# Other places in SBUF for the operands of a hybrid encoder layer's matmuls

## The chip, the core and the metric

The kernel runs on one core of a Trainium2 chip. The metric is the device time of one execution in microseconds (us); lower is better. Engines are named as in the profile: PE is TensorE's matmul, PEld its weight load, DVE VectorE, ACT ScalarE, POOL GpSimd, SP SyncE.

## What is computed

One layer over a sequence of 512 tokens of width 1024, all in float32. Three parts follow each other, each added to the residual stream `x`; shift, scale and gate of each part come from a conditioning vector.

```python
def swiglu(h, w_in, w_out):
    gate, up = jnp.split(h @ w_in, 2, axis=-1)
    return (jax.nn.silu(gate) * up) @ w_out
...
h = modulate(rmsnorm(x, norm_ffn1[l]), sh1, sc1)
x = x + 0.5 * g1[:, None, :] * swiglu(h, w_ffn1_in[l], w_ffn1_out[l])
h = modulate(rmsnorm(x, norm_mix[l]), sh2, sc2)
qa, ka, va, qb, kb, vb, ga, gb = jnp.split(h @ w_in[l], SPLIT_POINTS, axis=-1)
...
ya = window_gqa_sink(qa, ka, va, sink_a[l]) @ w_branch_a[l]
...
yb = ob @ w_branch_b[l]
merged = jax.nn.sigmoid(ga) * ya + jax.nn.sigmoid(gb) * yb
x = x + g2[:, None, :] * (merged @ w_out[l])
h = modulate(rmsnorm(x, norm_ffn2[l]), sh3, sc3)
x = x + 0.5 * g3[:, None, :] * swiglu(h, w_ffn2_in[l], w_ffn2_out[l])
```

The hidden width of each SwiGLU is 2816. `window_gqa_sink` is attention within a window of 128 with 8 query heads and 2 key heads; `ob` comes from a differential attention of 4 heads over all 512 tokens.

## The kernel before

**Products.** Every large product is made of float32 values that are split into a high and a low part; a product is three matmuls (high by high, high by low, low by high), the lines 456 to 458 in `two` and 173 to 175 in `mm3`. In the first FFN from its fourth pair of column blocks on, and in nearly all of the second, the products of blocks follow Strassen's scheme in seven products of 2 x 2 blocks: a `Unit` has the quarters `a11`, `a12`, `a22` of its weights and the sums `s1` to `s4`, and the operand's quarters `b11` to `b22` with the sums `n1`, `n2`, `t3`, `t4` (`OPERAND` says which goes with which; `n1` goes with `s1`). Such matmuls move 256 columns; the plain ones move 512. A product takes 6 matmuls for each step of depth, so 24 at depth 4.

**Places of the weights.** The split weights lie in two tiles, `high` and `low`, of five slots each. `high_low` hands the slots out in turn; a set is one slot's pair. A set starts, in float32 values, at `i * 1024 + min(i, 2) * GAP + aside` for slot `i`, where `GAP` is 64 and the caller gives `aside`: 16 (`ASIDE`), 24 (`TURN`), 64 (`FAR`) or 0. So slots 2, 3 and 4 are 1024 apart, and a set with an `aside` ends in the next slot's first values.

**Places of the operands.** Operands lie in tiles called `b8` (`b` in the profile) and, some, in `u4` tiles (`u`) and in `ka`. The first FFN's `n1` is in two `u4` tiles (line 605); in the second FFN `n1` is in `u4` too, and of what the second output product reads, the last places are `ka` and `u4`. In bytes of a partition, modulo 256, `high`, `low`, `b8` and `ka` tiles start at 64 and `u4` tiles at 160 (from the order and the sizes in which the pool's tiles are laid out).

**The difference.** While TensorE streams one matmul's operand, the next matmul's weights are loaded. The text calls "difference" the start of those weights less the start of that operand, in bytes modulo 256. An `aside` of 16 under a `b8` operand gives 64; under `n1` in `u4` tiles it gives 224; `TURN` gives 96 under a `b8` operand, `aside` 0 or `FAR` gives 0. Where the operand moves out of `high` and `low` and the weights are in `b8` (the projections of lines 1192 to 1213), the sign turns: `aside` 16 gives 192.

**Order of work.** The first FFN's input products alternate with its output products, which move 512 columns (`Out1`, FAR): output chunks start near 110, 181, 252 and 324 us, and behind each of the first three the next unit's product `s2` is the first of 256 columns. The last four output columns (`LAST_1`) are done by halves of 256 columns, from 340 us, then the first three gates, whose weights are in `u4` tiles (to 377 us). Then come the projections of the mixers, gates and attention (to about 645 us; the window mixer's keys and queries by `project_pairs`, lines 1198 to 1215, from 454 to 499 us), among which small transposes (line 1270) are strewn; then the rest of the branch products, the mixer's output columns (`MIX_ASIDES`; the last two by halves, from 701 us), and the second FFN from 713 us. In that the first unit is `Plain` (two halves of a plain product, sets `a11` and `a21` at `TURN`), beside it `lead`, and from 743 us on units in Strassen's scheme, with two `out_unit`s from 812 us on, two from 927 us on and two at the end. TensorE's order is written out by hand in the FFNs and at the boundaries between the parts; elsewhere a scheduler orders each engine's instructions by priority and by what must wait for what.

Of the kernel before, what the change touches and what calls it, by code (L numbers as in the profile page):

```python
# [18 lines left out]
P = 128  # L19
# [77 lines left out]

RAW, HILO, F2 = 5, 5, 8

ASIDE, TURN, GAP = 16, 24, 64  # L100

FAR = 64


BRANCH_ASIDES = (ASIDE, TURN, ASIDE, ASIDE), (ASIDE,) * 4
MIX_ASIDES = 0, 0, 0, 0, 0, 0, ASIDE, ASIDE

CHUNKS = (range(0, 6), range(6, 12), range(12, 16), range(16, 22))
PLAIN, LAST_1 = 3, 4
# [24 lines left out]
def layer(ctx: ExitStack, tc: tile.TileContext, a: dict):  # L134
# [13 lines left out]
    def xt():  # L148
        return sbuf("x", [P, T], F32, 8)
# [16 lines left out]
    def keep(shape, nm, dt=F32):  # L166
        return sb.tile(shape, dt, name=nm, tag=nm, bufs=1)
# [28 lines left out]
    def high_low(n=1024, aside=0, holder=None):  # L196
        while turn[0] % HILO in holders:
            turn[0] += 1
        i = turn[0] % HILO
        turn[0] += 1  # L200
        if holder:
            holders[i] = holder
        i = i * 1024 + min(i, 2) * GAP + aside
        return tuple(t[:, i : i + n] for t in parts)

    def let_go(holder):
# [24 lines left out]
    sub8, lam_s, nlam = (keep([P, n], nm) for nm, n in (("sub8", 1), ("lam_s", 2), ("nlam", 1)))  # L231
    rqa, ccol = keep([P, NT, 8], "rqa"), small(NC)
    x = [xt() for _ in range(NC)]
    parts, modv = [], []
    for nm, n in (("high", 6), ("low", 0)):
        parts.append(keep([P, HILO * 1024 + 2 * GAP + ASIDE], nm, F32R))
        modv += [keep([P, NC], f"mod{v}") for v in range(n)]

    def load_by(t, src, n):
# [9 lines left out]
        return w  # L249


    begin, begins, norms = keep([P, 6 * NC], "begin"), {}, {SC1: NORM1, SC2: NORM2, SC3: NORM3}

    def mod_begin(v):
        if v in (SH1, SH2, SH3):
# [204 lines left out]
    class Unit:  # L460
# [12 lines left out]
        MAKE = {"s1": 5, "a11": 3, "a12": 2, "s2": 4, "s4": 2, "s3": 2, "a22": 3}  # L473
        asked, length = ("s1", "a11", "a12", "a22"), 1.0

        in_order = turned = by_columns = ()
        spare, roomy, apart, more = ("s1",), (), (), {"s1": ("s2", "a11"), "s2": ("s4", "a12"), "a11": ("s3", "a21")}

        def place(self, q):
# [14 lines left out]
        def prepare(self, q):  # L494

            if q in self.ready:
                return
            self.ask(q)
            n = self.depth * 2 * P
            if q in self.apart:  # L500
                both = b8().rearrange("p a b -> p (a b)")
                hi, lo = both[:, 0:n], both[:, 1024 : 1024 + n]
            else:
                hi, lo = high_low(n, TURN if q in self.turned else ASIDE, (self, q))
            t = self.at[q]
            with tc.issue_after(copied[0]) if q in self.in_order and copied else nullcontext():
                split_from(hi, lo, t)
            self.ready[q] = hi, lo
            if q in self.more:
                s, src = self.more[q]  # L510
                G.dma_start(t, self.srcs[src], accum_op=ALU.add)
                self.at[s] = t
# [103 lines left out]
    cact = [sbuf("ka", [P, D], F32, 1)]  # L616
    hh, hl = new_h()
    modv += [keep([P, NC], f"mod{v}") for v in range(len(modv), 9)]
    nc.scalar.dma_start(ccol, a["c"])
    tc.keep_in_program_order(nc.scalar.dma_start(par, a["par"]))  # L620
    for c in range(NC):
# [2 lines left out]
    with tc.manual_schedule(engines=BOUND | {mybir.EngineType.SP, mybir.EngineType.Pool}):  # L624
# [24 lines left out]
        def first_loads(k):  # L649
            n = 1 if k else 2  # L650
            scale = mod_load(SC1, k, n=n)
            if k == 0:
                kept.append(keep([P, NT], "pos", I32))
            shift = mod_load(SH1, k, n=n) if k == 0 else None
            raw = sbuf("raw", [P, 1024], F32, RAW)
            load_by(raw, a["w1s"][k], n)
            w1[k] = [scale, shift or mod_load(SH1, k), raw]
# [227 lines left out]
    def in_unit1(p):  # L885
        srcs = {q: a["w1u"][p - PLAIN, i] for i, q in enumerate(("a11", "a12", "a21", "a22"))}
        u = Unit(srcs, 4, h1_operand, in_post1, p % 2)
        u.p, u.in_order = p, ('s2', 's4')
        return u

    class Out1:
# [17 lines left out]
        def prepare(self, m):  # L909
            if m not in self.ready:  # L910
                self.ask(m)
                aside = FAR if not self.by_halves(m) else TURN if m < NC - LAST_1 + 2 else ASIDE
                if self.final and m == 0:
                    while turn[0] % HILO != 1:
                        turn[0] += 1
                t = self.ready[m] = high_low(self.depth * P, aside, (self, m))
                with tc.issue_after(copied[0]):
                    split_from(*t, self.at[m])
# [196 lines left out]
    def load_main(src, aside=0):  # L1115

        raw = sbuf("raw", [P, 1024], F32, RAW)
        nc.sync.dma_start(raw, src)
        hi, lo = high_low(aside=aside)
        halves = slice(0, 512), slice(512, 1024)  # L1120
        for j in halves:
            S.copy(hi[:, j], raw[:, j])
        for j in halves:
            S.activation(lo[:, j], raw[:, j], AF.Identity, scale=-1.0)
        G.dma_start(lo, src, accum_op=ALU.add)
        return hi, lo
# [68 lines left out]
                    yield MM3 * n / T  # L1195
        then(out)

    def project_pairs(srcs, then):

        n = 2 * P  # L1200
        out = [bank("acc") for _ in range(2)]
        for u, src in enumerate(srcs):
            wh, wl = load_main(src, ASIDE)
            for t in range(NT):
                ht = slice(t * P, (t + 1) * P)
                po = out[t // 2][:, t % 2 * n : (t % 2 + 1) * n]
                for i in range(4):
                    k = 4 * u + i
                    w = slice(i * n, (i + 1) * n)
                    first, last = k == 0 and t % 2 == 0, k == NC - 1 and t % 2 == 1  # L1210
                    PE.matmul(po, hh[k][:, ht], wh[:, w], start=first, stop=False, skip_group_check=True)
                    PE.matmul(po, hh[k][:, ht], wl[:, w], start=False, stop=False, skip_group_check=True)
                    PE.matmul(po, hl[k][:, ht], wh[:, w], start=False, stop=last, skip_group_check=True)
                    yield MM3 / 2
        then(out)
# [11 lines left out]
    def gates(more=lambda: True):  # L1227
        while gate_next[0] < 16 and more():
            j = gate_next[0]
            gate_next[0] += 1  # L1230

            wh, wl = load_main(a["w_gate"][j], ASIDE * (j == EARLY_A))
            out = bank("acc")
            for k in range(NC):
                o = k * P
                mm3(out, wh[:, o : o + P], wl[:, o : o + P], hh[k], hl[k], k == 0, k == NC - 1)
                yield MM3
            gate_end(j, out)
# [423 lines left out]
            turns["w"] = (b, g * nk + kc + 1)  # L1662


    def branch(w, j0, o_h, o_l, then, load, r=FULL[0], asides=(0, 0, 0, 0)):
        for u in range(4):
            with tc.issue_after(banded_last[0]):
                wh, wl = load(w[u], aside=asides[u])
            for i in range(2):
                j = 2 * u + i  # L1670
                g = f2()[:, r]
                nc.sync.dma_start(g, gate_scr[j0 + j][:, r])
                y = bank("acc")[:, r]
                for k in range(4):
                    o = k * 256 + i * P
                    mm3(y, wh[:, o : o + P], wl[:, o : o + P], o_h[:, k, r], o_l[:, k, r], k == 0, k == 3)
                    yield MM3 * (r.stop - r.start) / T
                then(j, g, y, r)

    def main():  # L1680
# [4 lines left out]
        while later or asked:  # L1685
            column(later)
        tables_a()
        yield from project_pairs([a["w_kva"][u] for u in range(2)], keys_a)
        for g in range(2):
            yield from project_pairs([a["w_qa"][2 * g + u] for u in range(2)], lambda ps, g=g: queries_a(ps, g))  # L1690
        yield from gates(lambda: done["b"] < NT)
# [19 lines left out]

        for i, r in enumerate(HALVES):
            line.drain(lambda: done["a"] >= 2 * i + 2)
            yield from branch(a["w_ya"], 0, *wa["o"], then_b, load_halves, r, BRANCH_ASIDES[i])

    mix = []
    line.run(main())
# [85 lines left out]
    def out_unit(part, g, final):  # L1803
        def post(c, v, u):
            n, t = int(c[1]) - 1, int(c[2]) - 1
            for j in range(2):
                m = 4 * g + 2 * n + j
                xr = x[m][:, HALVES[t]]
                V.scalar_tensor_tensor(xr, v[:, j * H : (j + 1) * H], modv[G3][:, m : m + 1], xr, ALU.mult, ALU.add)
                if final:  # L1810
                    nc.sync.dma_start(a["out"][m][:, HALVES[t]], xr)

        r = slice(part.start * 2 * P, part.stop * 2 * P)
        srcs = {q: a["w2o"][g, i][:, r] for i, q in enumerate(("a11", "a12", "a21", "a22"))}
        return Unit(srcs, len(part), act_operand, post, g)

    units = [in_unit(p) for p in range(NH)]

# [19 lines left out]
            V.scalar_tensor_tensor(g, g, -1.0, self.bank[1, t], ALU.mult, ALU.mult)  # L1838

    plain = units[0] = Plain(units[0].srcs, 4, h_operand, None, 0)  # L1840
    plain.turned = ("a11", "a21")
    lead = units[1]
    lead.spare, lead.roomy, lead.apart = ("s1", "a11", "a12"), ("a22",), ("s1", "a12")
    for u in units[1:]:
        u.in_order = ("s2", "s3", "s4", "a22") if u is lead else ("s1", "s2", "s3", "s4", "a22")
    units[2].MAKE = {**Unit.MAKE, "s2": 3}
    lead.tags = {"w": "acc", "v": "tp"}
    with tc.manual_schedule(engines={mybir.EngineType.Pool}):
        for u, q in ((plain, "a11"), (plain, "a21"), (lead, "a11")):
# [249 lines left out]
```

## Time and profile before

| | |
|---|---|
| runs | 1039.71 us median of 3 (1039.4 to 1041.84) |
| the profiled execution | 1039.97 us, of which the span 1038.2 |
| PE busy | 1030.8 us (99%), granted clock 1.00 |
| PEld busy | 951.1 us (92%) |
| DVE, ACT, POOL busy | 786.9, 583.9, 162.5 us |
| DMA | 220.92 MB, 213 GB/s over the span |

The span reaches from the first to the last instruction in the profile. Matmuls overlap, and their ends are modelled, so a matmul's duration in the profile is longer than the distance from its start to the next one's start. What a stretch costs is therefore read from starts: in the view of windows each row gives a stretch (from and to, in us from the span's start), its length, then PE's busy time with the count of matmuls that touch the stretch, the granted clock, the DMA engines' share and GB/s. In the timeline a row is start, length, engine, line and operation.

### The profile page before, as it was taken

The page shows a single profiled execution, that of the slowest core. Times are in us where ns is not written, and L with a number is a line of the kernel's source. Part 1 is how long each engine was busy: PE and PEld are TensorE (multiplying, and loading weights), DVE is VectorE, ACT ScalarE, POOL GpSimd, SP SyncE. Part 2 cuts the span into 40 slices and gives each one's busy share as a digit, 9 for nine tenths or more (in the row PEclk, how much of TensorE's full clock was granted, in tenths as well). Part 3 has the DMA queues.
Part 4 walks back from the last instruction along what each step waited for, and adds up shares of the span by engine and source line. Part 5 has one row for each costly group of instructions (what it writes and reads, how often), then busy time and mean ns, then how long its engine had stood idle before and what let it go on. Part 6 is the DMA issues. An engine that isn't in the chain of part 4 may idle for free.

```text
span 1038.2 us, 18851 instructions
## 1 busy us (share of the span) xinstructions
PE 1030.8 (99%) x7346; PEld 951.1 (92%) x7346; DVE 786.9 (76%) x1456; ACT 583.9 (56%) x1014; POOL 162.5 (16%) x190
## 2 busy tenths in 40 slices
PE   9999999999999999999999999999999999999998
PEld 7789899899999998899888888989999999999998
DVE  7786667567796679859782598976899777877877
ACT  6665335244364343667785856525867546654553
POOL 1101110110110100543333101001112112112210
PEclk9999999999999999999999999999999999999999
DMA  9977787966884459796737944974498998989974
GB/s 360 356 238 203 233 231 209 257 166 205 253 203 133 152 192 410 236 288 139 186 69 190 254 134 151 364 252 104 94 237 191 243 229 207 224 223 214 211 156 112
DMA packets 70377, 220.92 MB, mean 213 GB/s; under 512 B 8464, under 2 KB 13200, under 8 KB 70288
## 3 DMA queue, kind: packets, MB, share of 16 engines
q1 hardware_dynamic: 47808, 146.52, 39.0%
q0 software_dynamic: 19344, 68.70, 35.9%
q10 hardware_dynamic: 3136, 4.51, 1.2%
q8 instruction: 57, 0.93, 0.3%
q14 instruction: 32, 0.26, 0.1%
HBM read 209.46 MB, written 10.23 MB: 212 GB/s over the span
## 4 chain that ended last, share of the span: by engine, by line
PE 94%; DMA 2%; DVE 2%; ACT 2%; issue 0%; SPq 0%; DVEq 0%; ACTq 0%
PE acc L457 7%; PE acc L458 7%; PE acc L456 7%; PE sc L457 6%; PE sc L458 6%; PE sc L456 6%; PE sc L173 5%; PE sc L174 5%; PE sc L175 5%; PE acc L173 5%; PE acc L175 5%; PE acc L174 5%; PE tp L1270 2%; DMA raw<-w1s 2%; PE acc L1192 2%; PE acc L1194 2%
## 5 line engine op out<-in xcount | busy, mean ns | idle before, releaser
L189 ACT CAST high<-raw 128x1024 fp32r<-128x1024 f32 (+2 forms) x176 | 158.2, 913 | 152.9 <-PE sc L174 40.4
L189 DVE TENSOR_TENSOR low<-raw,high 128x1024 fp32r<-128x1024 f32 (+2 forms) x176 | 183.2, 1050 | 42.1 <-ACT high L189 40.8
L456 PE MATMUL acc<-b,high 128*128 128x256 f32 x508 | 140.9, 277 | 0.0
L457 PE MATMUL acc<-b,high 128*128 128x256 f32 x508 | 140.7, 277 | 0.1
L458 PE MATMUL acc<-b,low 128*128 128x256 f32 x508 | 140.6, 277 | 0.0
L457 PE MATMUL sc<-b,high 128*128 128x256 f32 x500 | 138.2, 276 | 0.0
L456 PE MATMUL sc<-b,high 128*128 128x256 f32 x500 | 138.1, 276 | 0.0
L458 PE MATMUL sc<-b,low 128*128 128x256 f32 x500 | 138.1, 276 | 0.0
L189 ACT CAST high<-u 128x1024 fp32r<-128x1024 f32 (+1 forms) x73 | 75.5, 1035 | 50.5 <-PE sc L174 20.2
L189 DVE TENSOR_TENSOR low<-u,high 128x1024 fp32r<-128x1024 f32 (+1 forms) x73 | 87.6, 1200 | 20.4 <-ACT high L189 18.8
L173 PE MATMUL sc<-b,high 128*128 128x512 f32 (+1 forms) x272 | 97.5, 358 | 0.0
L174 PE MATMUL sc<-b,high 128*128 128x512 f32 (+1 forms) x272 | 97.2, 357 | 0.0
L175 PE MATMUL sc<-b,low 128*128 128x512 f32 (+1 forms) x272 | 97.1, 357 | 0.0
L457 PEld LDWEIGHTS acc<-b,high 128*128 128x128 f32 x508 | 95.5, 188 | 0.4 <-DVE b L1883 0.3
L456 PEld LDWEIGHTS acc<-b,high 128*128 128x128 f32 x508 | 95.5, 188 | 0.3 <-ACT f L534 0.2
L458 PEld LDWEIGHTS acc<-b,low 128*128 128x128 f32 x508 | 95.4, 188 | 0.0
L458 PEld LDWEIGHTS sc<-b,low 128*128 128x128 f32 x500 | 93.9, 188 | 0.0
L456 PEld LDWEIGHTS sc<-b,high 128*128 128x128 f32 x500 | 93.9, 188 | 0.0
L457 PEld LDWEIGHTS sc<-b,high 128*128 128x128 f32 x500 | 93.9, 188 | 0.0
L173 PE MATMUL acc<-b,high 128*128 128x512 f32 (+1 forms) x240 | 89.0, 371 | 0.0
L175 PE MATMUL acc<-b,low 128*128 128x512 f32 (+1 forms) x240 | 86.7, 361 | 0.0
L174 PE MATMUL acc<-b,high 128*128 128x512 f32 (+1 forms) x240 | 86.5, 361 | 0.0
(397 smaller groups left out, 2715.9 us busy)
## 6 DMA issues: line engine op xcount, KB each, us to landing
u<-w_mod SPq DMA_DIRECT2D x38, 512.0 KB, 8.3
b<-w_mod SPq DMA_DIRECT2D x32, 512.0 KB, 5.5
raw<-w2i SPq DMA_DIRECT2D x31, 512.0 KB, 5.4
u<-w2i POOLq DMA_DIRECT2D x31, 512.0 KB, 6.7
raw<-w1u SPq DMA_DIRECT2D x24, 512.0 KB, 7.1
u<-w1u POOLq DMA_DIRECT2D x24, 512.0 KB, 7.1
raw<-w1o SPq DMA_DIRECT2D x24, 384.0 KB, 4.4
raw<-w_gate SPq DMA_DIRECT2D x16, 512.0 KB, 5.2
```

Source lines behind the costliest of these rows:

```text
L173: PE.matmul(out, wh, xh, start=first, stop=False)
L174: PE.matmul(out, wh, xl, start=False, stop=False)
L175: PE.matmul(out, wl, xh, start=False, stop=last)
L189: last = S.copy(hi, src), V.tensor_tensor(lo, src, f(hi), ALU.subtract)
L456: PE.matmul(out, wh[:, s], xh, start=first and j == 0, stop=False, skip_group_check=True)
L457: PE.matmul(out, wh[:, s], xl, start=False, stop=False, skip_group_check=True)
L458: PE.matmul(out, wl[:, s], xh, start=False, stop=last and j == 1, skip_group_check=True)
L1192: PE.matmul(out[t][:, 0:n], hh[k][:, ht], wh[:, o : o + n], start=k == 0, stop=False)
L1194: PE.matmul(out[t][:, 0:n], hl[k][:, ht], wh[:, o : o + n], start=False, stop=k == NC - 1)
L1270: PE.transpose(tp[:, j * P : (j + 1) * P], src, ident)
```

## The change

It moves operands and weights in SBUF; no instruction is added or taken away, and what is computed stays.

- Small tiles are added or widened ("pad1", "pad2", `begin`, "pos"), so that `u4` tiles start where `b8` tiles do, at 64 modulo 256, and `high` and `low` start at 0. The DMA scratch goes from 4096 to 2048 bytes.
- The slots of `high` and `low` are all 1088 values apart, and 16 is added to every `aside`. So an `aside` of 16 still gives 64 under `b8`, and now under `n1` too; 0 still gives 0.
- `FIRST`, -8, gives 224. It goes to: `s1` of the first Strassen unit (224 before as well, being `n1`'s), the sets behind the 512 columns of the first FFN's output (`s2`, 64 before), the first set of the window branch's first half (64 before), the second to last mixer output column (64 before), `a11` of the second FFN's third unit (64), and `s1` of the first output unit of each of the second FFN's first two parts (64).
- `ENTRY`, 32, gives 128: the first of the four last output columns of the first FFN (96 before); the other three have 64 (96 for one of them before). `TURN` is gone: the second FFN's `a11` and `a21` of `Plain` and a set of the window branch go from 96 to 64.
- In `project_pairs` the first set gives 224 and the others 64 (192 before); one gate goes from 64 to 0; the first three gates, with their weights in `u4`, go from 96 to 0; products of attention that read `u4` tiles go from 160 to 0.

```diff
-ASIDE, TURN, GAP = 16, 24, 64
+ASIDE, FIRST, GAP = 16, -8, 64
+ENTRY = 32
...
-BRANCH_ASIDES = (ASIDE, TURN, ASIDE, ASIDE), (ASIDE,) * 4
-MIX_ASIDES = 0, 0, 0, 0, 0, 0, ASIDE, ASIDE
+MIX_ASIDES = 0, 0, 0, 0, 0, 0, FIRST, ASIDE
...
-        i = i * 1024 + min(i, 2) * GAP + aside
+        i = i * (1024 + GAP) + ASIDE + aside
...
+    keep([P, 48], "pad1")
...
-        parts.append(keep([P, HILO * 1024 + 2 * GAP + ASIDE], nm, F32R))
+        parts.append(keep([P, HILO * (1024 + GAP) + ASIDE], nm, F32R))
...
-    begin, begins, norms = keep([P, 6 * NC], "begin"), {}, {SC1: NORM1, SC2: NORM2, SC3: NORM3}
+    begin, begins, norms = keep([P, 6 * NC + ASIDE], "begin"), {}, {SC1: NORM1, SC2: NORM2, SC3: NORM3}
...
-                hi, lo = high_low(n, TURN if q in self.turned else ASIDE, (self, q))
+                hi, lo = high_low(n, self.asides.get(q, ASIDE), (self, q))
...
+    keep([P, 40], "pad2")
...
-                kept.append(keep([P, NT], "pos", I32))
+                kept.append(keep([P, 2 * NC], "pos", I32)[:, 0:NT])
...
+        if p == PLAIN:
+            u.asides = {"s1": FIRST}
+        elif 2 * p in [c.start for c in CHUNKS[1:]] or p == PLAIN + 1:
+            u.asides = {"s2": FIRST}
...
-                aside = FAR if not self.by_halves(m) else TURN if m < NC - LAST_1 + 2 else ASIDE
+                aside = (ENTRY if m == NC - LAST_1 else ASIDE) if self.by_halves(m) else FAR
...
-    def project_pairs(srcs, then):
+    def project_pairs(srcs, then, first=False):
...
-            wh, wl = load_main(src, ASIDE)
+            wh, wl = load_main(src, -FIRST if first else -ASIDE)
+            first = False
...
-            wh, wl = load_main(a["w_gate"][j], ASIDE * (j == EARLY_A))
+            wh, wl = load_main(a["w_gate"][j])
...
-            yield from branch(a["w_ya"], 0, *wa["o"], then_b, load_halves, r, BRANCH_ASIDES[i])
+            yield from branch(a["w_ya"], 0, *wa["o"], then_b, load_halves, r, (ASIDE if i else FIRST,) + (ASIDE,) * 3)
...
-        return Unit(srcs, len(part), act_operand, post, g)
+        u = Unit(srcs, len(part), act_operand, post, g)
+        if g == 0 and not final:
+            u.asides = {"s1": FIRST}
+        return u
...
-    plain.turned = ("a11", "a21")
...
+    units[2].asides = {"a11": FIRST}
...
-    nc = bacc.Bacc("TRN2", target_bir_lowering=False, num_devices=1, dynamic_dma_scratch_size=4096)
+    nc = bacc.Bacc("TRN2", target_bir_lowering=False, num_devices=1, dynamic_dma_scratch_size=2048)
```

The order of the instructions stays on SP and POOL. Since a set no longer ends in the next slot, the scheduler issues some instructions of ACT, DVE and, once, PE in another order. On PE that is in `project_pairs`, among the query products of the window mixer (`high`, `low` are the moving weights, `b` the normalised input, `acc` the sum, `tp` the bank of a transpose). Before:

```order
L1212 MATMUL acc_4520<-low,b_265_3237 128x256
L1213 MATMUL acc_4520<-high,b_267_3239 128x256
L1211 MATMUL acc_4520<-high,b_265_3237 128x256
L1270 MATMUL tp_4544<-ident,f_404_4256 128x128 x4
L1212 MATMUL acc_4520<-low,b_265_3237 128x256
L1213 MATMUL acc_4520<-high,b_267_3239 128x256
```

After (lines and numbers are those of the changed kernel):

```order
L1219 MATMUL acc_4522<-low,b_265_3239 128x256
L1220 MATMUL acc_4522<-high,b_267_3241 128x256
L1277 MATMUL tp_4546<-ident,f_404_4258 128x128 x4
L1218 MATMUL acc_4522<-high,b_265_3239 128x256
L1219 MATMUL acc_4522<-low,b_265_3239 128x256
L1220 MATMUL acc_4522<-high,b_267_3241 128x256
```

Four transposes stand one matmul earlier. On ACT a part of the copies into `high` and `low` moves among the copies of the projections' results (`f`), here near the loads ahead of the window mixer's projections. Before:

```order
L1122 CAST high<-raw_4359 128x512
L1124 ACTIVATE low<-raw_4359 128x512 x2
L1122 CAST high<-raw_4359 128x512
L1122 CAST high<-raw_4414 128x512 x2
L1124 ACTIVATE low<-raw_4414 128x512
L1291 COPY f_395_4223<-acc_4059 128x512
L1124 ACTIVATE low<-raw_4414 128x512
```

After:

```order
L1128 CAST high<-raw_4361 128x512 x2
L1130 ACTIVATE low<-raw_4361 128x512 x2
L1130 ACTIVATE low<-raw_4416 128x512
L1128 CAST high<-raw_4416 128x512 x2
L1130 ACTIVATE low<-raw_4416 128x512
L1298 COPY f_395_4225<-acc_4061 128x512
L1298 COPY f_396_4227<-acc_4062 128x512
```

The copies of one set stand together, and one copy of a result no longer stands between the two halves of a set.

More of the change, by code (lines that the diff above doesn't have):

```diff
@@ L474, in layer @@
         asked, length = ("s1", "a11", "a12", "a22"), 1.0
[L476 removed]
+        in_order, by_columns, asides = (), (), {}
         spare, roomy, apart, more = ("s1",), (), (), {"s1": ("s2", "a11"), "s2": ("s4", "a12"), "a11": ("s3", "a21")}
@@ L1662, in window_out, with branch @@
             turns["w"] = (b, g * nk + kc + 1)
-    def branch(w, j0, o_h, o_l, then, load, r=FULL[0], asides=(0, 0, 0, 0)):
+    def branch(w, j0, o_h, o_l, then, load, r=FULL[0], asides=(0,) * 4):
         for u in range(4):
@@ L1687, in main @@
         tables_a()
-        yield from project_pairs([a["w_kva"][u] for u in range(2)], keys_a)
+        yield from project_pairs([a["w_kva"][u] for u in range(2)], keys_a, True)
         for g in range(2):
```

## The prediction

> **What bounds the kernel now.** I read the page first, then the windows of TensorE, cut so that each holds 24 matmuls of 256 columns, then its timeline at the places where the pace changes. The page:
>
> ```profile
> PE 1030.8 (99%) x7346; PEld 951.1 (92%) x7346; DVE 786.9 (76%) x1456; ACT 583.9 (56%) x1014; POOL 162.5 (16%) x190
> PEclk9999999999999999999999999999999999999999
> PE 94%; DMA 2%; DVE 2%; ACT 2%; issue 0%; SPq 0%; DVEq 0%; ACTq 0%
> ```
>
> TensorE is busy 99% of the span at the full clock, and the chain that ended last is 94% PE. So a change of places can pay in little but the pace of the matmuls. Their mean durations hide that pace, because the matmuls overlap. A window from the start of one matmul to the start of the 24th after it shows it (the count in brackets includes those that lap over its edges):
>
> ```profile
> 142.57:145.40 2.83, 2.83 (x26) 1.00 0.91 262
> 82.48:85.30 2.82, 2.82 (x25) 1.00 0.77 110
> 85.30:88.02 2.72, 2.72 (x26) 1.00 1.03 205
> 307.52:310.24 2.72, 2.72 (x27) 1.00 0.77 243
> 316.06:318.89 2.83, 2.83 (x27) 1.00 0.22 22
> 1031.44:1034.16 2.72, 2.72 (x27) 1.00 0.55 188
> ```
>
> These are the same 24 matmuls at the same clock, and they take 2.72 us (113.3 ns each) or 2.82 to 2.83 (about 118 each), 4% more. DMA load doesn't sort them: at a share of 1.03 the pace is fast, at 0.22 slow. The places do, together with what ran ahead. "Difference" below is the start of the weights that are loaded next, less the start of the operand that streams meanwhile, modulo 256 bytes. Difference 64 runs at either pace: fast at 307.52, slow at 142.57, which is the first set behind 512-column matmuls. At 82.48 the first set behind 512 columns has difference 224 (it reads n1), and it is slow too; but the set behind it, at 64, is fast. In the timeline of TensorE the last rows ahead of 316 show what else makes 64 slow:
>
> ```profile
> 315.45 0.28 PE L458 MATMUL acc<-b,low 128*128 128x256 f32 x1
> 315.72 0.38 PE L456 MATMUL acc<-b,high 128*128 128x256 f32 x1
> 315.94 0.28 PE L457 MATMUL acc<-b,high 128*128 128x256 f32 x1
> ```
>
> Two starts come 0.27 and 0.22 us apart instead of 0.11, and from there the same difference that was fast at 307.52 stays slow to the end of its stretch. I read this as: 64 has two paces, holds the one it has, is put on the slow one by 512 columns or a stall, and on the fast one by a set at another difference. The window at 1031.44 lies over 400 matmuls behind the last set of another difference and is still fast. [...]
>
> **The change part by part.** *n1 at 64.* Today n1's tiles give 224. All such sets, seven in the first block and fifteen in the second (of 24, 6 or 30 matmuls, 264 in all), first and last with the sums:
>
> ```profile
> 93.48:96.29 2.81, 2.81 (x27) 1.00 0.88 334
> ...
> 295.74:298.55 2.81, 2.81 (x27) 1.00 0.65 186
> sum 19.64, PE 19.64; mean PE 2.81
> ...
> 754.46:757.26 2.80, 2.80 (x27) 1.00 1.04 217
> ...
> 983.96:986.76 2.80, 2.80 (x26) 1.00 0.78 182
> sum 30.85, PE 30.85; mean PE 2.06
> ```
>
> At the fast pace the first seven would take 7 x 2.72 = 19.04 us, a gain of 0.60; the others 264/24 x 2.72 = 29.92, a gain of 0.93. This holds only if their neighbours are on the fast pace, and today it is n1 itself that puts them there. That is what the sets at 224 behind 512 columns replace.
>
> *First sets behind 512 columns, 64 to 224.* 2.83 us becomes what 82.48 shows, 2.82: nothing by itself, and the set behind it fast, as at 85.30.
>
> *New sets at 224 in the second block, and the end of the mixers.*
>
> ```profile
> 746.16:748.90 2.74, 2.74 (x26) 1.00 0.87 142
> 811.76:814.48 2.72, 2.72 (x26) 1.00 0.96 212
> 926.52:929.24 2.72, 2.72 (x27) 1.00 0.99 227
> 649.04:651.86 2.82, 2.82 (x26) 1.00 1.01 395
> 703.73:706.56 2.83, 2.83 (x27) 1.00 0.48 49
> 708.75:710.11 1.36, 1.36 (x13) 1.00 1.04 199
> ```
>
> The first three rows go from 64 to 224, so to the 2.80 of n1 in midstream: +0.23 us in all. The row at 649.04 (96 today, 64 then, behind a set at 224) and the one at 703.73 (64, on the slow pace since the 512 columns; then behind a set at 224) go to 2.72: -0.21. Of 14 matmuls that go to 224, 12 have the last row; they are fast today (1.36 us for 12, 113 ns each) and lose at most 14/24 x 0.10, +0.05.
>
> *First gates, 96 to 0.* They take their weights from u tiles, which now stand as the b tiles do:
>
> ```profile
> 372.59:375.41 2.82, 2.82 (x27) 1.00 0.37 100
> 729.44:732.32 2.88, 2.88 (x26) 1.00 0.28 108
> ```
>
> The second row is a set at 0 today, of weights in a b tile under a b operand. So 24 gate matmuls go from 2.82 to 2.88; 107 of them, 107/24 x 0.06 = +0.27. The window products of attention go from 160 to 0, where both ends are already slow: nothing.
>
> *Where 64 is new and its pace is open.*
>
> ```profile
> 339.95:348.42 8.47, 8.47 (x74) 1.00 0.63 228
> 354.61:357.33 2.72, 2.72 (x26) 1.00 0.25 96
> 460.15:462.15 2.00, 2.00 (x20) 1.00 1.05 408
> 487.58:490.40 2.82, 2.82 (x25) 1.00 0.29 68
> 644.46 0.60 PE L1270 MATMUL tp<-ident,x 128*128 128x128 f32 x4
> 645.01:646.78 1.77, 1.77 (x17) 1.00 0.53 150
> 501.60:506.68 5.08, 5.08 (x24) 1.00 0.64 141
> 117.17:122.61 5.44, 5.44 (x25) 1.00 0.92 224
> 723.91:726.73 2.82, 2.82 (x26) 1.00 0.86 309
> 737.84:743.29 5.45, 5.45 (x51) 1.00 0.11 20
> ```
>
> The end of the first FFN (339.95: 72 matmuls at 8.47 us, 8.16 if fast) gets 128 for its first 18, a difference that no row shows: between 0 and 0.16 per 24 above fast, by the rows of 2.72 and 2.88. If the 54 behind them, and as many in the second half, turn fast, 0.6 is gained; if nothing turns, up to 0.2 is lost. I take -0.2, since half of its sets stand behind stalls. The key and query projections of the window mixer (454 to 499) go from 192 to 224 for one set and then 64. Their 17 matmuls at 460.15 (2.00, 1.93 if fast) follow that set: -0.08. Behind them come transposes, again and again. At 354.61, behind the row sums' small matmuls, 64 is fast; behind transposes (644.46) the next set at 64 is slow (15 matmuls at 645.01 in 1.77 us, 1.70 if fast), and so is 723.91. Some 210 matmuls at 0.1 per 24 are -0.9 if all turn fast; I take -0.15 for the whole part, the transposes being the nearer row. One gate (501.60: 21 matmuls of 512 columns, 5.08 us with a restart behind a transpose) goes from 64 to 0. At 0 the 24 at 117.17 take 5.44, which makes 4.76 for 21; how much of the 0.32 between them is the restart's the row doesn't tell, so the gain is between 0 and 0.3, and I take -0.08. In the second block's first unit the sets at 96 go to 64, today between slow (723.91) and fast (737.84): -0.2 or +0.2, taken as nothing.
>
> *The rest.* The slots of the sets stand further apart, so that no set laps into the next slot, and a few copies of ScalarE and VectorE are issued in another order; the chain gives these engines 2% each: within 0.3 either way, taken as nothing. The DMA scratch is halved; POOL isn't in the chain at all, so a later issue is covered by the five slots and the loads that are asked for several sets ahead, and if that cover went, it would show as PE idle. I take nothing.
>
> **Sum.** -0.60 - 0.93 + 0.23 - 0.21 + 0.05 + 0.27 - 0.2 - 0.15 - 0.08 = -1.6 us, against the profiled execution of 1039.97 (span 1038.2, so 1.8 outside it): 1038.4. That execution lies 0.26 above the median of the runs, 1039.71; so I forecast 1038.1. A measurement of this kernel tells about 0.3% from no change, 3.1 us: below 1036.6 or above 1042.8.
>
> **The rivals.** *Restarts come out fast* (14%). If 64 behind transposes and stalls took the fast pace, as at 354.61, the open places would give 0.6 - 0.2 and 0.9 - 0.15 more, the second block's first unit 0.2 and the stretch behind 316.06 its 7.3 us x 4% = 0.3: 1038.1 - 1.7 = 1036.4. For it: the restarts at 354.61 and 708.75 are fast today. Against it: those at 142.57, 316.06, 645.01 and 723.91 are slow.
>
> *The set at 224 does not turn the pace* (8%). Behind 512 columns the only set at 224 today reads u tiles; if one that reads b tiles left 64 slow, everything behind it would be slow to the end of its stretch, for n1 no longer turns it. The first block has 145.40 to 180.95, 216.44 to 252.00 and 276.61 to 323.48, 118 us, of which 7 are slow already: 111 x 4% = 4.5 us, 1042.6. With the second block from 748.90 on, 285 us x 4% = 11.4 more: 1054. The point that decides is the first window behind each such set, and it is the same mechanism that shows 2.72 at 85.30, so I give it little.
>
> *Places do nothing, or the difference isn't what counts* (8%): then 1039.7 stays. [...] Against it stand all pairs of rows above.
>
> *The reordered copies or the smaller scratch cost a stall* (8%): one stall like 315.45 costs 0.27 and turns the rest of its stretch slow, up to 2.5 us for a stretch of 63 us: 1040.6 at most.
>
> **How the numbers follow.** The forecast has 62%. The range takes the fast rival and half a microsecond for the scatter of medians, 1035.9, to a lost stretch, 1040.6; outside are the rival of 1042.6 and more, and the far end of the fast one. Faster by over 0.3%: most of the fast rival and a little of the forecast, 14%. Slower by over 0.3%: the rival at 224, and a little more, 9%. Within: 77%.
>
> **What would show it.** In the profile after: n1's sets at 2.72 per 24; the first set behind 512 columns at 2.82 and the next at 2.72; the first gates at 2.88; three sets at 2.80 in the second block. I am wrong if the window behind a set at 224 shows 2.83, if the long stretches of the second block leave 2.72, or if the copies' order opens a stall of TensorE that isn't there today.

## The result, and the profile after

The changed kernel takes 1037.15 us in the median of 9 runs (1036.54 to 1040.46), the kernel before 1039.71 in 9 beside it (1039.32 to 1041.84): a ratio of 0.9976, with a 95% interval of 0.9967 to 0.9984. That is 2.56 us, 0.24%, less than the 0.3% that the prediction set as its bound for telling a difference, though the interval leaves 1 out. The forecast was 1038.1 us. The profiled execution took 1036.79 us (span 1035.0), 3.18 less than the one before.

The page's first lines. Clock, engines and the shape of the chain are as before; PE is busy 2.3 us less:

```profile
PE 1028.5 (99%) x7346; PEld 949.4 (92%) x7346; DVE 787.0 (76%) x1456; ACT 583.8 (56%) x1014; POOL 163.2 (16%) x190
PEclk9999999999999999999999999999999999999999
PE 95%; DMA 2%; DVE 1%; ACT 1%; issue 0%; SPq 0%; DVEq 0%; ACTq 0%
```

The windows of TensorE, from and to in us, length, PE's busy time (count), clock, DMA share and GB/s. Each row is the same matmuls as a row of the prediction, by their place in the program, cut at their starts in this trace:

```profile
142.06:144.86 2.80, 2.80 (x25) 1.00 1.02 312
144.86:147.58 2.72, 2.72 (x26) 1.00 1.02 419
314.91:317.63 2.72, 2.72 (x26) 1.00 0.19 19
338.52:346.82 8.30, 8.30 (x74) 1.00 0.69 237
371.08:373.96 2.88, 2.88 (x26) 1.00 0.49 141
458.67:460.67 2.00, 2.00 (x19) 1.00 1.11 411
499.49:504.47 4.98, 4.98 (x25) 1.00 0.59 145
701.27:703.99 2.72, 2.72 (x27) 1.00 0.36 53
735.33:740.99 5.66, 5.66 (x51) 1.00 0.12 23
752.25:754.97 2.72, 2.72 (x27) 1.00 1.02 221
809.25:812.05 2.80, 2.80 (x26) 1.00 0.96 222
1028.26:1030.98 2.72, 2.72 (x26) 1.00 0.56 191
```

n1's sets are at 2.72 (144.86, 752.25). The first set behind 512 columns is at 2.80 (142.06), and n1 right behind it is fast. The new sets at 224 in the second block cost 2.80 (809.25 is one of the three), the first gates 2.88 (371.08), and the last stretch holds 2.72 to its end, over 900 matmuls behind the last set at 224. The end of the mixers (701.27) turned from 2.83 to 2.72, the end of the first FFN (338.52) went from 8.47 to 8.30, and the gate at 499.49 from 5.08 to 4.98. Three places are not as priced. Behind the stall that the prediction quoted at 315.45, difference 64 is now fast (314.91). The window mixer's projections (458.67 is their first set, still 2.00) gain in the sets further on. And `Plain`'s 48 matmuls at 735.33, fast before, are slow (5.66 for 5.45).

### The profile page after: what moved, and what is told of

Same layout as the page of the kernel before. It is cut to its first block, busy times and chain, and to the rows that moved or that the text cites. A ratio compares the mean times of both kernels' runs of the same rounds, so it can differ in the third digit from the quotient of the medians.

```text
span 1035.0 us, 18850 instructions
## 1 busy us (share of the span) xinstructions
PE 1028.5 (99%) x7346; PEld 949.4 (92%) x7346; DVE 787.0 (76%) x1456; ACT 583.8 (56%) x1014; POOL 163.2 (16%) x190
## 4 chain that ended last, share of the span: by engine, by line
PE 95%; DMA 2%; DVE 1%; ACT 1%; issue 0%; SPq 0%; DVEq 0%; ACTq 0%
PE acc L458 7%; PE acc L457 7%; PE acc L459 7%; PE sc L459 6%; PE sc L458 6%; PE sc L457 6%; PE sc L173 5%; PE sc L174 5%; PE sc L175 5%; PE acc L173 5%; PE acc L175 5%; PE acc L174 5%; PE tp L1277 2%; PE sc L186 2%; DMA raw<-w1s 2%; PE acc L1198 2%
## 5 line engine op out<-in xcount | busy, mean ns | idle before, releaser
L189 DVE TENSOR_TENSOR low<-raw,high 128x1024 fp32r<-128x1024 f32 (+2 forms) x176 | 183.1, 1050 | 41.2 <-ACT high L189 36.6
```

What stands on the lines that cost most here:

```text
L189: last = S.copy(hi, src), V.tensor_tensor(lo, src, f(hi), ALU.subtract)
```

## The experiments

The theory that came out of the two traces: difference 64 has two paces, 113.3 and 117.8 ns for a matmul of 256 columns, and holds the one it has; 512 columns leave it slow; a set at 224 leaves it fast; a stall starts it afresh on either. The rivals: it is the difference alone, or n1's own place, that is paid for; a stall always puts 64 on the slow pace (the prediction's reading); the time came from the reordered copies or the smaller scratch. The scratch has a run of its own below; the reordered copies have none.

**The sets behind 512 columns, taken back.** In the first FFN's three units behind 512 columns `s2` goes back to 64; all else stays as changed.

```diff
-            u.asides = {"s2": FIRST}
+            u.asides = {"s2": ASIDE}
```

> The changed kernel, but the three sets behind 512 columns in the first block stand at difference 64 instead of 224. Theory (64 has two paces, 512 columns put it on the slow one, only a set of another difference turns it): 64 is slow from there to the end of each of the three stretches, 312, 312 and 408 matmuls at 4.45 ns more each, so 4.6 us slower than the changed kernel, 1041.7 us; every 24 matmuls in 145 to 180 us take 2.83 us. Rival (each set costs what its own difference costs; 64 is cheap): the three sets gain 0.1 us each, 1036.9 us, and the stretches behind stay at 2.72.

1041.35 us (1040.72 to 1043.78), a ratio to before of 1.0021, interval 1.0011 to 1.003. Windows of the kernel without these sets: the second 24 matmuls at 64 behind 512 columns, and 24 near the end of the same stretch:

```profile
144.71:147.54 2.83, 2.83 (x26) 1.00 1.03 414
176.75:179.58 2.83, 2.83 (x27) 1.00 0.15 18
```

The slow pace now lasts to the end of the first two stretches, 312 matmuls each. In the third it lasts over 341, up to a forced wait at 318 us, the one that the prediction quoted at 315.45; the 67 behind it are fast. Against the changed kernel the three stretches take 1.39, 1.39 and 1.50 us more. Without its three sets at 224 the change would be a loss. The rival by which only the difference of a set itself counts falls: what these sets buy lies behind them.

**n1 alone.** The kernel before, with `u` tiles moved to where `b` tiles stand (so n1 at 64), no set at 224 in their stead, and the scratch at 2048.

```diff
+    keep([P, 40], "pad2")
...
-    nc = bacc.Bacc("TRN2", target_bir_lowering=False, num_devices=1, dynamic_dma_scratch_size=4096)
+    nc = bacc.Bacc("TRN2", target_bir_lowering=False, num_devices=1, dynamic_dma_scratch_size=2048)
```

> The kernel before with one thing of the change alone: n1's tiles moved so that they give 64 (with the DMA scratch at 2048 bytes); no set is put at 224. Theory: n1 was what turned 64 fast, so now the first block is slow from each 512-column stretch to the next (1270 matmuls, 4.5 us more than before) and the second block from the product at difference 0 near 743 us to the end (2508 matmuls, 10.1 us more than before), and the first gates cost 0.28 more: 15 us slower than before, 1054.6 us. Rival (each set costs what its own difference costs): 1.55 us gained, 0.28 lost, 1038.4 us.

1054.1 us (1053.76 to 1054.38), ratio 1.0135, interval 1.0118 to 1.0152, so 14.5 us more than before. Windows of that kernel: n1 in the first block, and sets at 64 in the second, early and at its end:

```profile
146.11:148.94 2.83, 2.83 (x27) 1.00 1.03 420
761.69:764.52 2.83, 2.83 (x27) 1.00 1.05 274
1045.30:1048.13 2.83, 2.83 (x27) 1.00 0.56 193
```

The part of the change that looks like its gain (n1 at the cheaper difference) costs 14.5 us when it is done alone, since nothing then takes 64 off the slow pace, in the second block over all 2500 matmuls. It is close to the 1054 that the prediction worked out for its second rival. These 14.5 us come from moved places; no view here shows where in the chip they arise.

**The other differences.** In the changed kernel six units of the second block take differences 0, 32, 96, 128, 160 and 192.

```diff
+    for i, by in ((3, 0), (5, 8), (6, 24), (7, 32), (9, 40), (10, 48)):
+        units[i].asides = dict.fromkeys(("a11", "a12", "a22", "s1", "s2", "s3", "s4"), by)
```

> The changed kernel with six units of the second block at other differences, each for 168 matmuls: 0, then a unit at 64, then 32, 96, 128, a unit at 64, 160, 192, then 64 to the end. It measures what each difference costs at length and which pace 64 takes behind 0, 128 and 192. Theory, from rows seen so far, per 24 matmuls: 0 2.88, 96 2.81, 128 2.89, 160 2.87, 192 2.82, 32 not seen (2.72 to 2.89); 64 slow (2.83) behind 0 as in the first unit of the second block, open behind 128 and 192; 1042.5 to 1045.7 us in all. Rival (only 64 and 224 differ, and the rest is chance): paces that don't sort by difference.

1042.91 us in one execution, from which all these rows come. Windows of 24 matmuls at, in order: 0; 64 behind 0; 64 behind 224; 32; 96; 128; 64, a single set behind 128; 64 behind the last set at 128; 160; 192; 64 behind 192:

```profile
777.03:779.91 2.88, 2.88 (x26) 1.00 0.98 265
797.14:799.97 2.83, 2.83 (x27) 1.00 0.63 219
814.08:816.80 2.72, 2.72 (x26) 1.00 1.06 253
855.02:857.86 2.84, 2.84 (x26) 1.00 0.91 273
874.95:877.83 2.88, 2.88 (x27) 1.00 0.40 156
895.04:897.89 2.85, 2.85 (x27) 1.00 0.42 157
909.27:912.10 2.83, 2.83 (x27) 1.00 1.01 262
914.95:917.67 2.72, 2.72 (x26) 1.00 0.36 143
972.33:975.21 2.88, 2.88 (x27) 1.00 0.89 272
992.33:995.05 2.72, 2.72 (x27) 1.00 0.94 252
1010.01:1012.73 2.72, 2.72 (x27) 1.00 0.91 148
```

Only 64 and 192 reach 2.72, and 192 has both paces as well, since it ran at 2.82 in the projections before. Difference 0 leaves 64 slow, as 512 columns (which are at 0 too) do; 224 leaves it fast; 128 has left it both ways. That "a set of another difference" makes 64 fast, as the prediction put it, was too wide.

**A stall, first try.** In the changed kernel one set's split is asked for later, so that TensorE would wait for it near 856 us.

```diff
+    units[5].MAKE = {**Unit.MAKE, "a12": 0}
```

> The changed kernel, with the weights of one product in the second block's sixth unit (a12) split only when they are due, so that TensorE has to wait for them once, some 1.5 us, near 856 us. No difference is changed. Theory: the wait puts 64 on the slow pace, 2.83 per 24, until the set at 224 near 924 us turns it back: 600 matmuls at 4.45 ns, 2.7 us, and with the wait 4.2 us more than the changed kernel, about 1041.3 us. Rival (a stall costs itself alone): 2.72 behind it, 1038.7 us.

1038.27 us in one execution. The wait did not come, since ScalarE and VectorE still finished the set in time; for its purpose the run tells nothing. But near 766 us two matmuls started 115 and 124 ns after the ones ahead instead of 113, and from there 64 is slow up to the set at 224 near 811, where it turns fast again. Windows behind the disturbance, of the set at 224, and behind that:

```profile
768.30:771.12 2.82, 2.82 (x26) 1.00 0.98 214
810.70:813.50 2.80, 2.80 (x26) 1.00 0.98 263
813.50:816.22 2.72, 2.72 (x26) 1.00 1.05 245
```

The 384 matmuls cost 1.7 us for a disturbance of 13 ns.

**Stalls, second try.** In seven units of the second block VectorE rewrites one column of a12's high part, by a chain of small operations behind the product ahead. What is computed stays.

```diff
+            if q in self.stalls:
+                hi, t = self.ready[q][0], small(1)
+                with tc.high_priority():
+                    V.tensor_scalar(t, last_po[0][:, 0:1], 0.0, None, ALU.mult)
+                    for _ in range(self.stalls[q]):
+                        V.tensor_scalar(t, t, 0.0, None, ALU.mult)
+                    V.tensor_tensor(hi[:, 0:1], f(hi[:, 0:1]), t, ALU.add)
+            last_po[:] = [po]
...
+    for n, i in enumerate((3, 4, 5, 6, 7, 9, 10)):
+        units[i].stalls = {"a12": n}
```

> The changed kernel with seven forced stalls: in seven units of the second block, the weights of one product (a12) are written once more in their first column (unchanged: plus zero times a sum of the product before), so that TensorE must wait for VectorE there, by a chain of 2 to 8 small operations. No difference is changed. Theory, mended after the last runs: a stall at 64 starts the pace afresh, and it comes out either fast or slow, 2.72 or 2.83 per 24 and nothing between, and stays so until the next stall or the next set at 224; some 0.7 to 1.5 us for each stall, and between 0 and 9 us for what is slow behind: 1043 to 1052 us. Rival (a stall costs itself alone, the flips seen came from elsewhere): 2.72 behind all seven, 1042 to 1047 us.

2065.98 us: a miss. The groups by line of that execution, with the same group's mean at 277 ns after the change, show matmuls at about half pace in every part, also in the first block, which this kernel does not touch:

```profile
L457 PE MATMUL acc<-b,high 128*128 128x256 f32 x508 | 219.2, 431 | 0.0
```

The view of windows reads a granted clock of 1.00 up to about 1941 us and of 0.56 from there to the end:

```profile
2000.00:2005.00 5.00, 5.00 (x28) 0.56 0.36 67
```

There matmuls of 256 columns start about 199 ns apart, against 113 to 118 at the full clock; ahead of it, where the view reads 1.00, they start 224 ns apart, so for that part it does not account for the pace. ScalarE and VectorE kept theirs: their copies out of `raw` took 911 and 1051 ns in the mean, against 914 and 1050 after the change. The same kernel was run once more:

> Changed kernel; in seven units of the second block VectorE rewrites one column of a12's high part behind the product ahead, by a chain of 2 to 8 small operations of about 0.19 us each, so TensorE should stall for 0.4 to 1.5 us in front of each, some 6.6 us in all. What is computed stays. Theory: a stall starts difference 64 afresh on either pace, so among the seven stretches behind the stalls some show 113.3 ns per matmul and some 117.8; a slow one costs 0.75 us for each unit up to the next set at 224, and the total is 1044 to 1048 us. Rival, the prediction's reading: a stall puts 64 on the slow pace; all seven stretches show 117.8, some 1500 matmuls of 4.45 ns make 6.7 us, and the total is about 1050 us.

1044.64 us. So the half pace was that execution's, not the kernel's; why the clock fell stays open. The time is within what the theory gave. The windows behind the seven stalls, in order:

```profile
784.30:787.02 2.72, 2.72 (x26) 1.00 1.08 209
804.60:807.32 2.72, 2.72 (x26) 1.00 1.09 211
862.11:864.94 2.83, 2.83 (x26) 1.00 1.02 211
882.47:885.29 2.82, 2.82 (x26) 1.00 1.04 228
902.84:905.56 2.72, 2.72 (x27) 1.00 1.08 209
981.60:984.32 2.72, 2.72 (x26) 1.00 0.69 201
1001.48:1004.31 2.83, 2.83 (x27) 1.00 0.54 152
```

Four come out fast and three slow, and of three other waits in this trace (434 ns at 765, 216 at 841, 113 at 1008) two fast and one slow. The reading that a stall always puts 64 on the slow pace falls, and with it the 1050 us that it gave. Of these ten, seven left 64 on the pace that it had ahead of them and three changed it, so they don't tell a pace that starts afresh from one that now and then flips.

**Eight sets more at 224.** In the changed kernel `s1` of each unit from the fourth on gives 224.

```diff
+    for i in range(3, NH):
+        units[i].asides = {"s1": FIRST}
```

> The changed kernel, with s1 of each of the second block's units from the fourth on at difference 224 (eight sets more; 24 matmuls each). Theory: the changed kernel's runs scatter by 1.2 us and more, the kernel's before by 0.4, because a chance wait turns 64 slow until the next set at 224, which used to be 168 matmuls away and is now up to 984; with a set at 224 in each unit the scatter goes back to about 0.5 us, at 8 x 0.083 = 0.66 us more than the changed kernel's best run: 1037.2 to 1037.8 us. Rival (the scatter comes from the waits themselves): as wide a scatter as the changed kernel's, median 1037.8 us.

1037.68 us (1037.28 to 1039.16), ratio 0.9979, interval 0.997 to 0.9987. The trace has the eight sets at +0.08 us each. The median is within what the theory gave, but 0.1 from the rival's; and the runs lie 1.9 us apart, not the 0.5 forecast, those of the changed kernel on this chip (next) 3.7.

**The changed kernel again**, on the same chip as the one above, to see how far its runs scatter.

> The changed kernel once more, for its scatter and a second profile. Theory: median 1037.1 us, runs from 1036.5 to above 1038, and in the profile whole stretches between two sets at 224 or stalls are either at 2.72 or at 2.83 per 24.

1038.5 us (1036.43 to 1040.15) over 11 runs, ratio 0.9981, interval 0.9971 to 0.999; the median is 1.4 above the one expected. Five runs lie at 1036.4 to 1036.9, six at 1038.5 to 1040.2.

The granted clock sorts most of them: it is 0.998 in the mean in five of the six upper runs and 1.00 in the sixth and in all of the lower. Over all kernels 18 runs read 0.998, among them five of the kernel before (1041.38 to 1042.67), and each lies at least 1.5 us above the lowest of its kernel on its chip. 0.002 of 1037 us is, as an estimate, 2.1 us, about what lies between the two groups. None of these runs was profiled, and the profiled executions in which 64 turned slow near 766 us read 1.00. So it is not shown that most upper runs are slow stretches of 64.

In the profiles of this family TensorE now and then waits at one place near 766 us, where a product needs a bank that ScalarE still copies. It took 11 to 1283 ns in eight profiles of kernels with the changed places, and was not there in the changed kernel's first, nor in that of the kernel before. Behind it 64 was fast in four of the eight and slow in the other four. The timeline of the longest, in the next kernel, with the idle time and its releaser in brackets:

```profile
766.00 0.28 PE L459 MATMUL sc<-b,low 128*128 128x256 f32 x1
767.39 0.39 PE L457 MATMUL acc<-b,high 128*128 128x256 f32 x1 [1.12 <-ACT f L535]
```

In that trace ScalarE had waited 1.70 us for an accumulating transfer into a `u` tile some ten us earlier, in the changed kernel's first 0.21: the likely source, not tested by itself.

**A set at 224 ahead of `Plain`.**

```diff
+    plain.asides = {"a11": FIRST}
```

> The changed kernel, with a11 of the second block's first unit (the plain one) at 224 too. There 64 runs slow behind a set at difference 0, 96 matmuls near 730 us, and some 70 more ahead of it. Theory: 6 of each 12 or 24 matmuls at 224 keep the rest fast: 0.3 to 0.5 us gained, 1036.7 us. Rival (64 is put back on the slow pace at each change between the two differences): nothing gained, 1037.1 us.

1037.47 us (1036.54 to 1040.16), ratio 0.9976, interval 0.9966 to 0.9987. Among sets at 0 a set at 224 doesn't reach far: it made its neighbours faster by 0.042 us at each of two places, and the 48 matmuls at 735.60 us stay slow at 5.65. The two expectations lie too close together for the time to tell them apart. The profiled execution, 1040.16, has the wait of 1.28 us above, and is slow from there to the set at 224 near 812.

**The smaller scratch alone**, in the kernel before.

```diff
-    nc = bacc.Bacc("TRN2", target_bir_lowering=False, num_devices=1, dynamic_dma_scratch_size=4096)
+    nc = bacc.Bacc("TRN2", target_bir_lowering=False, num_devices=1, dynamic_dma_scratch_size=2048)
```

> The kernel before with the DMA scratch at 2048 bytes and nothing else. Theory: the scratch is neither a gain nor the source of the changed kernel's scatter; 1039.7 us (1039.4 to 1040.0), runs spread as the kernel before's on the same chip, and no wait of TensorE in the profile near 766 us. Rival: the smaller scratch makes POOL's accumulating transfers land later, which opens the waits seen near 766 us in the changed kernel's profiles; then the runs fall in groups 1 to 2 us apart, with a median of 1040.2 or more.

1040.05 us, against 1040.1 of before on this chip: ratio 1.0, interval 0.9991 to 1.0009. The scratch neither gains nor costs. A short wait at the place near 766 us (0.1 us, at 768 in this kernel) is in this profile too, so the wait doesn't need the changed places; whether the scratch has a part in it, one profile of each doesn't tell, but the runs spread no wider than those of before (1039.46 to 1041.88, without one of 1133.86 at a granted clock of 0.85, against 1039.47 to 1041.98). Here 64 stayed fast behind the wait, and n1 at 224 came 47 matmuls later anyway.

**One more set at 224**, in the fourth unit only, just behind the place of the wait.

```diff
     units[2].asides = {"a11": FIRST}
+    units[3].asides = {"s1": FIRST}
```

> Changed kernel with one more set at 224, s1 of the second block's fourth unit, at about 770 us. Theory: the changed kernel's upper group of runs is a disturbance near 766 us that leaves 64 slow until the set at 224 near 809 us; the new set ends that after some 48 matmuls, so for 0.08 us the upper group comes down by up to 1.5 us: median 1036.9 us (1036.6 to 1037.6), no run above 1038.8 but by a longer wait. Rival: the groups come from elsewhere; runs spread as before, 1036.4 to 1040.2, with a median of 1037.2 to 1038.5.

1036.92 us (1036.67 to 1038.82) in 7 runs, ratio 0.9972, interval 0.9961 to 0.9984. Its profile has the wait (80 ns); the windows behind it, of the added set, of the next one, and of the one ahead of the next set at 224 near 809:

```profile
768.33:771.16 2.83, 2.83 (x27) 1.00 1.02 237
771.16:773.96 2.80, 2.80 (x26) 1.00 1.07 363
773.96:776.70 2.74, 2.74 (x26) 1.00 0.98 187
806.62:809.34 2.72, 2.72 (x26) 1.00 1.06 309
```

The wait put 64 on the slow pace, and the added set took it off, as the theory says; this profiled execution takes 1036.89. Two runs of the seven still lie at 1038.6 and 1038.8, so the upper runs are not gone. Their granted clock is 0.998, that of the other five 1.00, which speaks for the rival; neither was profiled. The intervals of this kernel and of the changed one overlap: it is no slower, and whether it is faster is not shown.

## Why the prediction was right, and where its terms were not

Matched matmul by matmul, the 3.18 us between the two profiled executions come out so:

| term | predicted, us | measured, us |
|---|---|---|
| n1 in the first block, in the second | -0.60, -0.93 | -0.60, -0.95 |
| three new sets at 224 | +0.23 | +0.22 |
| end of the mixers | -0.21 + 0.05 | -0.14 |
| first gates | +0.27 | +0.27 |
| end of the first FFN | -0.2 | -0.26 |
| projections of the window mixer | -0.15 | -0.68 |
| one gate | -0.08 | -0.11 |
| `Plain` | 0 | +0.22 |
| first sets behind 512 columns | 0 | -0.10 |
| the stretch behind 314.57 | 0 | -0.28 |
| up to 82 us, ahead of all that is changed | 0 | -0.38 |
| the rest | 0 | -0.38 |

*What bounds it* held: the places set the pace, at the same clock and load, and kernels with nothing but places (and the scratch, which does nothing) moved range over 17 us, from 1036.9 to 1054.1.

*n1, the sets at 224, the gates* held to 0.02 us each, since each had a row of its own difference at its own pace. The condition set to n1's gain, neighbours on the fast pace, is what the first two experiments show. (The window at 1031.44 that the prediction quotes for a lasting pace starts 394 matmuls behind n1, not over 400.) The rest has one part that the sum left out: before, the first matmuls behind an n1 set were slow too (up to 123 ns from start to start), 0.28 us over 23 places.

*The projections* were the term that was mis-sized. The whole part, first before and then after:

```profile
454.49:500.90 46.41, 46.41 (x385) 1.00 0.78 196
```

```profile
453.07:498.80 45.73, 45.73 (x386) 1.00 0.80 197
```

It gained 0.68 of the 0.9 that the prediction gave as its bound. I took the transposes as restarts to the slow pace because the nearest row, behind 644.46, was slow. That row, from other places, did not tell: of the twelve stretches behind transposes, by their matmuls of 256 columns alone, seven came out 0.04 to 0.20 us shorter and five within 0.01. The stretch behind the forced wait near 314 us is the same error. It was slow before, 7.66 us, and took 7.38 after:

```profile
315.94:323.60 7.66, 7.66 (x66) 1.00 0.52 154
```

```profile
314.79:322.17 7.38, 7.38 (x67) 1.00 0.51 159
```

Neither is a throw that falls anew in each execution. The second profile of the changed kernel has both parts as the first:

```profile
453.38:499.11 45.73, 45.73 (x386) 1.00 0.77 196
315.09:322.47 7.38, 7.38 (x66) 1.00 0.53 160
```

Of the nine profiles at full pace of the changed kernel and its variants, seven have the projections at 45.72 to 45.76 us (two at 45.92 and 46.04), and all nine the other part at 7.38. With n1 moved alone it is 7.38 too, though 64 came to the wait on the slow pace; with the smaller scratch alone it is as before:

```profile
320.34:327.72 7.38, 7.38 (x66) 1.00 0.52 160
315.87:323.52 7.65, 7.65 (x66) 1.00 0.51 154
```

So behind these restarts, which come in every profile, the outcome mostly went with the places, while behind the waits for ScalarE near 766 us, whose length changes, both outcomes occur. What decides it is open, and in the projections no run separates the new differences from the new order of copies and transposes.

So the step that failed is "is put on the slow one by 512 columns or a stall": 512 columns do, a stall may. The rival "restarts come out fast" had the mechanism half right: many did, and its 1036.4 is near the lower runs. `Plain` came out slow where it was fast before, in all nine profiles, which the prediction had left open at 0.2 either way, and did.

*The rest, no stall from copies or scratch.* Two of the three rows of TensorE's waits (total, times, longest, us) after the change:

```profile
PE acc L705 <- ACT b L692: 1.3, 1, 1.3
PE tp L742 <- POOL sm L738: 0.2, 1, 0.2
```

The first stood at 2.1 before and at 2.4 in the changed kernel's second profile. The second, at 12 us, is not in the list before, nor in that second profile. So these waits, all within the first 30 us, change from run to run, and no stall came to stay. The 0.38 us up to 82 us, where difference 0 stayed 0, are of that kind: in the changed kernel's second profile the same matmul starts 0.30 us later than in its first, and over the twelve profiles at full pace it starts between 81.7 and 82.3 us. That part of the 3.18 us is luck.

That profiled execution also escaped the wait near 766 us, and the median of its runs lies 0.36 us above it. With the 0.26 us by which the profiled execution before lies above its own median, 3.18 us between the profiles are 2.56 between the medians. The range of the forecast, 1035.9 to 1040.6, holds the runs of both groups.

*What stays open*: what in the chip makes two paces; why 128 has left 64 both ways; what decides the pace behind a restart; what the reordered copies do by themselves; and what the upper runs at a granted clock of 0.998 hold.

## What to carry to other kernels

Where a stream of matmuls runs at 100% busy and full clock, measure the distance from start to start at every combination of places, and look for stretches where one combination shows two values. Here 64 showed two, 2.72 and 2.83 us for 24, so it was the history that was paid for, and one set in front of a long stretch was worth more than a good place for each set: three sets at 224 were worth 4.3 us (1.39 + 1.39 + 1.50) and cost nothing (2.80 us, against 2.82 to 2.83 at 64 in the same place). Before a set that looks expensive is moved, ask what it does for the sets behind it, and don't carry the pace behind a restart from one layout to another: here it mostly repeated from run to run, and changed when the places did.

## What the runs showed of the hardware

- At full clock a matmul of 256 columns took 113.3 or 117.8 ns from start to start at differences of 64 and, over two kernels, of 192; 116.7 at 224, 118.3 at 32, 118.8 at 128, 120.0 at 0 and 160, and 117.5 (before) or 120.0 at 96, all by windows of 24.
- Each of the two paces sustains itself: fast over 924 matmuls to the end of the changed kernel, slow over 2500 when n1 alone was moved. A disturbance of 13 ns was enough to leave it (the first try at a stall), and a wait of 434 ns kept it. Behind the forced wait near 314 us 64 was fast in all ten profiles at full pace with the moved `u` tiles and slow in the two without.
- In the profile before, the weights of the matmul that starts at 85.42 us begin to load at 85.31, 0.01 us behind the start of the matmul ahead of it (85.30): these two are what "difference" is taken between.
- One execution ran at about half the pace throughout, 431 ns for 277 in the same group of matmuls; the granted clock read 0.56 in its last 123 us, and 1.00 ahead of that at a pace no better (224 ns from start to start against 199): a single odd time is worth a second run before it is explained.
